# The channel stage of a 2-D Fourier mix computed once for both halves of its frequencies, with its product moved to GpSimd, inside a large transformer block in 32-bit arithmetic

## The chip, the cores and the metric

One core of a Trainium2 chip. The metric is the device time of one execution in microseconds (us). The engines are called as in the profile: PE (TensorE matmul), PEld (its weight loads), DVE (VectorE), ACT (ScalarE), POOL (GpSimd), SP (SyncE, which only issues transfers).

## The reference

One layer on 512 tokens of width 2048, with 256 context tokens. A normed and modulated input is projected to queries, keys, values, gates and the input of a Fourier branch; attention and Fourier mix run side by side, and their results are gated, merged, projected and normed. What the change touches is the Fourier branch:

```python
def _fourier_mix(u):                       # u: 512 tokens x 512 channels
    ug = u.reshape(b, n, 4, 128)           # four groups of 128 channels
    y = jnp.fft.fftn(ug, axes=(1, 3), norm="ortho").real
...
y_b = (_fourier_mix(u_b) * jax.nn.silu(z_b)) @ w_pb
```

`norm="ortho"` divides by the root of 512 x 128, which is 256. With A the transform over tokens (real part Ar, imaginary part Ai, up to sign), C and S the cosine and sine tables over channels, the real part at token frequency f is C Ar(f) - S Ai(f). The input is real, so at 512 - f it is C Ar(f) + S Ai(f).

## The kernel before

All matrix products are done on numbers split into a high part (rounded to the matmul's 32-bit input format) and a low part (the rest): `split_from` copies the high part on ACT and subtracts on DVE (L180, L181), and `mm3` issues three matmuls per product, high x high, high x low, low x high (L338, L339, L340). Most lines of the profile are such splits: `whi`, `wlo` are a weight's parts, `s` those of sums of the input's blocks (S4, Z and S among them), `ah`, `al` those of the token transform.

Weights are streamed. SP loads raw blocks `wr`; four chains R0 to R3 take further blocks by accumulating transfers on POOL's queue (L291) or by additions on DVE (`R<-R,wr`, L268). The program is a list of stages:

1. A start stage computes the Fourier input u and its gate input z_b with the weights as they arrive. `keep` puts the sums into the tile `part`; for z its rows 4 to 7, the last additions being L659.
2. The channel stage, the subject here. `halves` forms even and odd combinations of u's tokens. `tokens(g)`, one call for each of four channel groups, is the transform over tokens: 12 matmuls, 6 for even and 6 for odd frequencies, into PSUM tiles named `pb`, then the splits into `ah` and `al`. `positions(g)` is the transform over channels: 8 matmuls with `ah` and 4 with `al`, 256 columns each, into a PSUM tile `pd`. They are the cosine and sine terms of frequencies 0 to 255, and then once more those of 256 down to 1 with the sine's sign turned, for the other half. DVE multiplies the sum by 1/256 and by silu(z) in one instruction (L944), over z's place in `part`. `gate_b(g)` has made silu(z) before: a sigmoid on ACT (L949), a product on DVE (L950). Two stores (`b_d<-part`, L966) on POOL's queue then put the result in memory, for a later stage.
3. Eight groups of seven products each, P1, Q5, P2, Q6, P7, Q3, Q4 (a Strassen-like scheme: seven block products in place of eight). A product has four pieces; a piece is a weight block, split, and 12 matmuls into one of the PSUM pairs `x`, `y` or `banks`. `Group.run` goes through them. Groups 0 to 2 give queries and gates, group 3 uses a sigmoid for gates (L1182). The first product's sum is copied to `ev` by ACT (L1113); the tiles `ev` lie where `part` was.

The order of PE is written out by hand in the stages 1 and 2 (`tc.manual_schedule`); the other engines' orders come from a scheduler, held by `issue_after`, which `behind(...)` wraps: what stands inside it comes after the named instructions in its engine's order. In the channel stage, `split_piece` of the first weight blocks is put behind the low half of group g (`low[g]`), so that the splits of R0 to R2 stand between the groups' work.

Of the kernel before, what the change touches and what calls it, by code (L numbers as in the profile page):

```python
# [10 lines left out]
F32 = mybir.dt.float32  # L11
# [7 lines left out]
P = 128  # L19
# [25 lines left out]
RAW = 4  # L45

HL, MORE_HL = 3, 2
EVEN = 258

# [73 lines left out]
def block_kernel(ctx, tc, xT, ctx_rows, ctx_toks, x, c_row, w_ss, w_gate, vecs, qkg, rope, dft_c, dft_s,  # L123
# [32 lines left out]
    def uid(s):  # L156
        cnt[0] += 1
        return f"{s}{cnt[0]}"
# [20 lines left out]
    def split_from(src, hi, lo):  # L179
        first = nc.scalar.activation(hi, src, ACT.Copy)  # L180
        return first, nc.vector.tensor_tensor(lo, src, hi.bitcast(F32), op=ALU.subtract)  # L181
# [16 lines left out]
    def stream(key, src, *a, **k):  # L198
        todo.append(Piece(key, src if isinstance(src, list) else [src], *a, **k))
# [136 lines left out]
    def mm3(o, ah, al, bh, bl, start, stop, cont=False):  # L336

        nc.tensor.matmul(o, ah, bh, start=start, stop=False, skip_group_check=cont)  # L338
        nc.tensor.matmul(o, ah, bl, start=False, stop=False, skip_group_check=cont)  # L339
        nc.tensor.matmul(o, al, bh, start=False, stop=stop, skip_group_check=cont)  # L340
# [25 lines left out]

    for p in start_pieces():
        if p[2:5:2] == (KK - 4, 0):
            stream(("dfts", 0), dft_s[:, : 2 * EVEN], 2 * EVEN, 2, "raw")
# [143 lines left out]
    with tc.issue_after(nc.scalar.activation(ce, cvt, ACT.Exp, scale=-1.0).ins):  # L513
# [6 lines left out]
    fch = ppool.tile([P, 2, 3 * P], F32R, name="fch")  # L520
    fsq = [ppool.tile([P, 2, 2, EVEN], F32R, name="fsq0")]
    rx = pap.tile([P, T], F32, name="rx")
    wacc = bank3()
    def warm(n, src):
# [371 lines left out]
    fsq.append(fnp.tile([P, 2, 2, 256], F32R, name="fsq1"))  # L896
    split_table(1)

    def halves(a):
# [17 lines left out]

    def tokens(g):

        ah, al = (fnp.tile([P, 2, 257], F32R, tag=n, bufs=2, name=uid(n)) for n in ("ah", "al"))  # L920
        c = slice(P * g, P * g + P)
        for e in range(2):
            n = fsq[e].shape[-1]
            acc = bank()
            for a in range(2):
                mm3(acc[:, :n], uh[:, a, e, c], ul[:, a, e, c], fsq[e][:, 0, a, :], fsq[e][:, 1, a, :], a == 0, a == 1)
            k = slice(e, 257 - e, 2)
            low[g] = split_from(acc[:, :n].rearrange("p (r f) -> p r f", r=2), ah[:, :, k], al[:, :, k])[1]
        AH[g] = ah, al

    def positions(g):

        ah, al = AH.pop(g)
        acc = bank2()
        steps = [(256 * q, P * (r and 1 + q), (slice(0, 256) if q == 0 else slice(256, 0, -1)), r)
                 for q in range(2) for r in range(2)]
        for n, (o, t, k, r) in enumerate(steps):
            for m, i in enumerate((0, 1)):
                nc.tensor.matmul(acc[:, o : o + 256], fch[:, i, t : t + P], ah[:, r, k], start=n == m == 0, stop=False,
                                 skip_group_check=True)  # L940
# [3 lines left out]
        nc.vector.scalar_tensor_tensor(part[:, 4 + g, :], acc, 1.0 / 256.0, part[:, 4 + g, :], op0=ALU.mult, op1=ALU.mult)  # L944

    def gate_b(g):
        z = part[:, 4 + g, :]
        e = fnp.tile([P, T], F32, tag="sil", bufs=1, name=uid("e"))
        nc.scalar.activation(e, z, ACT.Sigmoid)  # L949
        nc.vector.tensor_tensor(z, z, e, op=ALU.mult)  # L950
# [444 lines left out]
    for g, kind in enumerate(KINDS):  # L1395
        if g == 3:
            jobs += [lambda: None] * 12 + [context_norm, lambda: None, lambda: None, context_spread]
        elif g == KV:
            while jobs:
                job()  # L1400
            assert not any(p[2] == "raw1" for e in ahead for p, _ in e.raws)
        elif g == KV + 1:
            qzs.close()
            gvs, gvp = region("gvp", "right", reuse_waits="tile")
            hl_pools += range(MORE_HL)
        group = Group(g, forms, new_ev, {"qz": qz_done, "kv": kv_done, "gate": gate_done}[kind], {"a": "x", "b": "y", "c": "x"})
        if g == KV:
            group.more = Context()
        for name in ONE_GROUP:
            if (g, name) in ((0, "Q4"), (KV + 1, "P1")):  # L1410
                assert not any(p[2] == "raw0" for e in ahead for p, _ in e.raws)
                load_row(int(g > 0))
            elif (g, name) == (1, "Q5"):
                silu_of_row(0, flat(new_ev()))
            if (g, name) == (0, "P7"):
                raw_pools.remove((rp, 1, "raw0", 1))
            if (g, name) == (0, "Q5"):
                more_hl.append(1)
# [24 lines left out]
    gvs.close()  # L1443
    evs.close()

# [543 lines left out]
def _constants():  # L1989
    pos = np.arange(T)  # L1990
    inv = (THETA ** (-np.arange(32, dtype=np.float64) / 32)).astype(np.float32)
    ang = np.stack([(pos // GRID).astype(np.float32)[:, None] * inv,
                    (pos % GRID).astype(np.float32)[:, None] * inv], axis=1)
    ang = ang.astype(np.float64)
    cos, sin = np.cos(ang), np.sin(ang)
    cos = np.stack([cos, cos], axis=2).reshape(T, HD)
    sin = np.stack([-sin, sin], axis=2).reshape(T, HD)
    rope = np.stack([cos, sin]).reshape(2, 4, P, HD).transpose(2, 0, 1, 3).astype(np.float32)
    a = 2 * np.pi * (np.outer(np.arange(P), np.arange(P)) % P) / P
    dft_c = np.concatenate([np.cos(a), -np.sin(a), np.sin(a)], axis=1).astype(np.float32)  # L2000
# [6 lines left out]
    dft_s = np.concatenate([table(np.arange(0, T // 2 + 1, 2)), table(np.arange(1, T // 2, 2))], axis=1)  # L2007
    return np.ascontiguousarray(rope), np.ascontiguousarray(dft_c), np.ascontiguousarray(dft_s)


# [58 lines left out]
```

## Time and profile before

| what | value |
| --- | --- |
| runs | 1290.64 us median of 3 (1289.82 to 1291.4) |
| profiled execution | 1290.61 us |
| its span | 1288.8 us, TensorE clock granted 0.998 of full speed |
| channel stage, PE | 144.60 to 156.13 us of the span |
| DMA | 319.14 MB, mean 248 GB/s |

The profile shows one execution. The span runs from its first to its last instruction; the runs' time has some 2 us more. In a line of the timeline stand the start, the duration, the engine, the line of code, the operation, what it writes and reads, its shape and, in brackets, how long the engine sat idle before and what ended that. A busy PE is not necessarily at its peak: matmuls are pipelined, so the time one takes of the engine is the distance between two starts, and the same holds for DVE and ACT.

### The profile page before, as it was taken

What the parts mean: (1) busy time and instruction counts of PE and PEld (TensorE: products, weight loads), DVE (VectorE), ACT (ScalarE), POOL (GpSimd) and SP (SyncE); (2) the same over time, 40 slices, a digit from 0 to 9 for tenths busy, and PEclk for the clock granted to TensorE, in tenths of its full rate; (3) what the DMA queues carried; (4) which work ended last, traced back from release to release, by engine and by line L of the source; (5) the groups of instructions that cost most, each with busy time, mean ns of one, the idle gap of its engine ahead of it and who ended that gap; (6) DMA issues with size and microseconds to landing.
All of it is one profiled execution on the core that took longest, in us unless ns stands there. A gap on an engine that the chain in (4) does not pass through costs nothing.

```text
span 1288.8 us, 17680 instructions
## 1 busy us (share of the span) xinstructions
PE 1272.9 (99%) x6586; PEld 1047.9 (81%) x6586; DVE 994.7 (77%) x1305; ACT 682.2 (53%) x1073; POOL 170.8 (13%) x222
## 2 busy tenths in 40 slices
PE   8999999999999999999999999999999999999997
PEld 5677887888888888888888888888888888888886
DVE  5767899889779787658587666788898777887677
ACT  5322654645556555444355544666667646464544
POOL 0000011111102011012031010012100211211210
PEclk9999999999999999999999999999999999999999
DMA  9998588888988988977879897578852989998986
GB/s 378 408 369 344 208 216 248 237 218 261 227 302 236 301 269 260 291 197 184 278 207 259 286 249 237 182 245 241 270 178 75 249 244 258 244 211 229 225 200 179
DMA packets 104486, 319.14 MB, mean 248 GB/s; under 512 B 9904, under 2 KB 33072, under 8 KB 100432
## 3 DMA queue, kind: packets, MB, share of 16 engines
q1 hardware_dynamic: 55056, 197.40, 42.3%
q0 software_dynamic: 27024, 98.19, 35.6%
q10 hardware_dynamic: 22320, 22.42, 5.1%
q8 instruction: 51, 0.84, 0.3%
q14 instruction: 35, 0.29, 0.1%
HBM read 283.36 MB, written 34.61 MB: 247 GB/s over the span
## 4 chain that ended last, share of the span: by engine, by line
PE 91%; DVE 3%; DMA 2%; ACT 2%; issue 1%; SPq 0%; ACTq 0%; DVEq 0%
PE banks L338 10%; PE banks L339 10%; PE banks L340 10%; PE x L340 9%; PE x L338 9%; PE x L339 9%; PE y L340 7%; PE y L339 7%; PE y L338 7%; PE banks L1543 2%; PE pd L566 2%; PE pb L338 1%; PE pb L339 1%; PE pb L340 1%; PE pc L338 1%; DMA wa<-in_w_ss 1%
## 5 line engine op out<-in xcount | busy, mean ns | idle before, releaser
L180 ACT ACTIVATE whi<-R 128x1024 fp32r<-128x1024 f32 x138 | 145.6, 1060 | 142.1 <-PE banks L340 55.3
L181 DVE TENSOR_TENSOR wlo<-R,whi 128x1024 fp32r<-128x1024 f32 x138 | 167.9, 1222 | 57.9 <-ACT whi L180 57.6
L181 DVE TENSOR_TENSOR wlo<-wr,whi 128x1024 fp32r<-128x1024 f32 (+1 forms) x122 | 147.2, 1214 | 63.1 <-ACT whi L180 63.1
L180 ACT ACTIVATE whi<-wr 128x1024 fp32r<-128x1024 f32 (+1 forms) x122 | 127.4, 1052 | 127.3 <-PE y L340 44.3
L338 PE MATMUL banks<-whi,s 128*128 128x512 f32 (+1 forms) x400 | 157.8, 394 | 0.9 <-DVE ev L1106 0.9
L339 PE MATMUL banks<-wlo,s 128*128 128x512 f32 (+1 forms) x400 | 155.8, 389 | 0.0
L340 PE MATMUL banks<-whi,s 128*128 128x512 f32 (+1 forms) x400 | 155.8, 389 | 0.0
L338 PE MATMUL x<-whi,s 128*128 128x512 f32 x352 | 137.1, 390 | 0.0
L340 PE MATMUL x<-whi,s 128*128 128x512 f32 x352 | 137.0, 389 | 0.0
L339 PE MATMUL x<-wlo,s 128*128 128x512 f32 x352 | 136.9, 389 | 0.0
L338 PE MATMUL y<-whi,s 128*128 128x512 f32 x316 | 123.1, 389 | 0.2 <-DVE cxe L1266 0.2
L339 PE MATMUL y<-wlo,s 128*128 128x512 f32 x316 | 123.1, 390 | 0.0
L340 PE MATMUL y<-whi,s 128*128 128x512 f32 x316 | 122.8, 389 | 0.0
L291 POOL DMA_DIRECT2D R<-in_w_g x64 | 56.0, 875 | 415.2 <-DVE wlo L181 212.6
L180 ACT ACTIVATE s<-wr 128x512 fp32r<-128x512 f32 (+2 forms) x93 | 60.9, 678 | 68.1 <-DMA wr<-cf_d 24.9
L338 PEld LDWEIGHTS banks<-whi,s 128*128 128x128 f32 x400 | 75.2, 188 | 16.6 <-DVE ev L1106 1.3
L181 DVE TENSOR_TENSOR s<-wr,s 128x512 fp32r<-128x512 f32 (+2 forms) x93 | 66.7, 750 | 28.3 <-ACT s L180 27.5
L340 PEld LDWEIGHTS banks<-whi,s 128*128 128x128 f32 x400 | 75.1, 188 | 15.3
L339 PEld LDWEIGHTS banks<-wlo,s 128*128 128x128 f32 x400 | 75.2, 188 | 13.6 <-DVE wlo L181 0.2
L340 PEld LDWEIGHTS x<-whi,s 128*128 128x128 f32 x352 | 66.1, 188 | 13.8
L339 PEld LDWEIGHTS x<-wlo,s 128*128 128x128 f32 x352 | 66.1, 188 | 13.7
L338 PEld LDWEIGHTS x<-whi,s 128*128 128x128 f32 x352 | 66.1, 188 | 13.6
(322 smaller groups left out, 2803.2 us busy)
## 6 DMA issues: line engine op xcount, KB each, us to landing
wr<-in_w_g SPq DMA_DIRECT2D x128, 512.0 KB, 5.8
R<-in_w_g POOLq DMA_DIRECT2D x64, 512.0 KB, 7.3
wa<-in_w_ss SPq DMA_DIRECT2D x31, 1024.0 KB, 9.7
R<-in_w_g SPq DMA_DIRECT2D x32, 512.0 KB, 6.0
wr<-in_w_gate SPq DMA_DIRECT2D x32, 512.0 KB, 5.1
wr<-in_w_o SPq DMA_DIRECT2D x24, 512.0 KB, 7.5
R<-in_w_o POOLq DMA_DIRECT2D x24, 512.0 KB, 9.2
wr<-in_w_pab SPq DMA_DIRECT2D x20, 512.0 KB, 6.0
```

What stands on the lines that cost most here:

```text
L180: first = nc.scalar.activation(hi, src, ACT.Copy)
L181: return first, nc.vector.tensor_tensor(lo, src, hi.bitcast(F32), op=ALU.subtract)
L291: nc.gpsimd.dma_start(chain[e.pc], e.nxt, accum_op=ALU.add)
L338: nc.tensor.matmul(o, ah, bh, start=start, stop=False, skip_group_check=cont)
L339: nc.tensor.matmul(o, ah, bl, start=False, stop=False, skip_group_check=cont)
L340: nc.tensor.matmul(o, al, bh, start=False, stop=stop, skip_group_check=cont)
L566: nc.tensor.matmul(acc[32 * j : 32 * j + 32], c2[:, n, :], w[:, k, :], start=n < 4, stop=n >= KK - 4)
L1543: nc.tensor.transpose(tp[:, k * P : (k + 1) * P], p[:, k * P : (k + 1) * P], ident)
```

## The change

- `positions` computes the cosine term and the sine term once, for 258 frequencies, in two accumulators `acc` (PSUM tiles `pb`): 4 matmuls with the high parts, then 2 with the low ones. ACT copies the sine term to `odd`; DVE subtracts it (columns 0 to 256) and adds it (255 columns, read backwards) to the cosine term, into `y`; GpSimd multiplies `y` by silu(z), over z's place.
- 1/256 goes into the cosine and sine tables, which lose the third block. Even and odd tables have 258 columns each.
- `tokens` takes its PSUM tiles from `bank2` (`pd`) and `bank3` (`pc`), where `positions` had `pd`.
- `gate_b` is one Silu on ACT, in place.
- The splits put behind `low[2]` and `low[3]` are now both behind `low[3]`, and the products P1 and Q5 of group 0 run in `behind((low[3],))`.

```diff
-EVEN = 258
+FREQ = 258
...
-            stream(("dftc", 0), dft_c, 3 * P, 1, "raw")
+            stream(("dftc", 0), dft_c, 2 * P, 1, "raw")
...
-            stream(("dfts", 1), dft_s[:, 2 * EVEN :], T, 2, "raw")
+            stream(("dfts", 1), dft_s[:, 2 * FREQ :], 2 * FREQ, 2, "raw")
...
-        ah, al = (fnp.tile([P, 2, 257], F32R, tag=n, bufs=2, name=uid(n)) for n in ("ah", "al"))
+        ah, al = (fnp.tile([P, 2, FREQ], F32R, tag=n, bufs=2, name=uid(n)) for n in ("ah", "al"))
         for e in range(2):
-            n = fsq[e].shape[-1]
-            acc = bank()
+            acc = (bank3 if e else bank2)()[:, :FREQ]
...
         ah, al = AH.pop(g)
-        acc = bank2()
-        steps = [(256 * q, P * (r and 1 + q), (slice(0, 256) if q == 0 else slice(256, 0, -1)), r)
-                 for q in range(2) for r in range(2)]
-        for n, (o, t, k, r) in enumerate(steps):
-            for m, i in enumerate((0, 1)):
-                nc.tensor.matmul(acc[:, o : o + 256], fch[:, i, t : t + P], ah[:, r, k], start=n == m == 0, stop=False,
+        acc = [bank()[:, :FREQ] for _ in range(2)]
+        for i, v in ((0, ah), (1, ah), (0, al)):
+            for r, o in enumerate(acc):
+                nc.tensor.matmul(o, fch[:, i, P * r : P * r + P], v[:, r, :], start=i == 0 and v is ah, stop=v is al,
                                  skip_group_check=True)
-        for n, (o, t, k, r) in enumerate(steps):
-            nc.tensor.matmul(acc[:, o : o + 256], fch[:, 0, t : t + P], al[:, r, k], start=False, stop=n == 3,
-                             skip_group_check=True)
-        nc.vector.scalar_tensor_tensor(part[:, 4 + g, :], acc, 1.0 / 256.0, part[:, 4 + g, :], op0=ALU.mult, op1=ALU.mult)
+        z = part[:, 4 + g, :]
+        y, odd = (fnp.tile([P, n], F32, tag=t, bufs=4, name=uid(t)) for t, n in (("y", T), ("odd", FREQ)))
+        nc.scalar.copy(odd, acc[1])
+        nc.vector.tensor_tensor(y[:, :257], acc[0][:, :257], odd[:, :257], op=ALU.subtract)
+        nc.vector.tensor_tensor(y[:, 257:], acc[0][:, 255:0:-1], odd[:, 255:0:-1], op=ALU.add)
+        nc.gpsimd.tensor_tensor(z, y, z, op=ALU.mult)
 
     def gate_b(g):
         z = part[:, 4 + g, :]
-        e = fnp.tile([P, T], F32, tag="sil", bufs=1, name=uid("e"))
-        nc.scalar.activation(e, z, ACT.Sigmoid)
-        nc.vector.tensor_tensor(z, z, e, op=ALU.mult)
+        nc.scalar.activation(z, z, ACT.Silu)
...
-        with behind((finals[-1], low[g])):
+        with behind((finals[-1], low[g if g < 2 else 3])):
...
-            group.run(name)
+            with behind((low[3],)) if (g, name) in ((0, "P1"), (0, "Q5")) else nullcontext():
+                group.run(name)
...
-    dft_c = np.concatenate([np.cos(a), -np.sin(a), np.sin(a)], axis=1).astype(np.float32)
+    dft_c = (np.concatenate([np.cos(a), np.sin(a)], axis=1) / 256.0).astype(np.float32)
```

What becomes of DVE's order in the channel stage: from its last addition to z to the second group's low halves. Before, each group's low halves stand behind a product with the sigmoid (`e`), and L944 multiplies `pd` by silu(z):

```order
L659 TENSOR_TENSOR part<-pc_1425,part 128x512
L950 TENSOR_TENSOR part<-part,e_1516 128x512
L181 TENSOR_TENSOR al_1440<-pb_1441,ah_1439 128x2x129
L181 TENSOR_TENSOR al_1440<-pb_1450,ah_1439 128x2x128
L950 TENSOR_TENSOR part<-part,e_1557 128x512
L181 TENSOR_TENSOR al_1460<-pb_1461,ah_1459 128x2x129
L181 TENSOR_TENSOR al_1460<-pb_1470,ah_1459 128x2x128
L181 TENSOR_TENSOR wlo_1554<-R_1339,whi_1553 128x1024
L944 SCALAR_TENSOR_TENSOR part<-pd_1482,part 128x512
```

After, in the same place (four low halves, a weight's split, then the subtraction and the addition of group 0):

```order
L659 TENSOR_TENSOR part<-pc_1425,part 128x512
L181 TENSOR_TENSOR al_1440<-pd_1441,ah_1439 128x258
L181 TENSOR_TENSOR al_1440<-pc_1450,ah_1439 128x258
L181 TENSOR_TENSOR al_1460<-pd_1461,ah_1459 128x258
L181 TENSOR_TENSOR al_1460<-pc_1470,ah_1459 128x258
L181 TENSOR_TENSOR wlo_1550<-R_1339,whi_1549 128x1024
L941 TENSOR_TENSOR y_1488<-pb_1480,odd_1489 128x257
L942 TENSOR_TENSOR y_1488<-pb_1480,odd_1489 128x255
```

The products with `e` and L944 are gone; the low halves follow each other directly, and the two y instructions stand where L944 stood.

POOL's order at that place, before:

```order
L766 DMA rot_d<-S_67 128x1024
L966 DMA b_d<-part 128x1024 x2
L1394 DMA qr<-rot_d 128x1024
L291 DMA R_1339<-in_w_g 128x1024
```

and after:

```order
L766 DMA rot_d<-S_67 128x1024
L943 TENSOR_TENSOR part<-y_1488,part 128x512
L943 TENSOR_TENSOR part<-y_1523,part 128x512
L963 DMA b_d<-part 128x1024
L943 TENSOR_TENSOR part<-y_1562,part 128x512
L943 TENSOR_TENSOR part<-y_1581,part 128x512
L963 DMA b_d<-part 128x1024
L1391 DMA qr<-rot_d 128x1024
L291 DMA R_1339<-in_w_g 128x1024
```

The four products stand in the queue ahead of the stores and of the transfers behind them.

DVE's order in the pieces of P7 and Q3 of group 0, some 50 us later. Names with their numbers (s40, s72: low halves for P7's last piece; s97, s128: for Q3's first; s333, in the changed order s341: the low half of the form S4). Before:

```order
L181 TENSOR_TENSOR s97_572<-wr317_1912,s95_571 128x2x256
L181 TENSOR_TENSOR s40_287<-wr316_1894,s38_286 128x2x256
L181 TENSOR_TENSOR s72_434<-wr316_1894,s70_433 128x2x256
L181 TENSOR_TENSOR s128_735<-wr317_1912,s126_734 128x2x256
L181 TENSOR_TENSOR wlo331_2022<-wr320_1932,whi330_2021 128x1024
L181 TENSOR_TENSOR s333_2038<-S30_67,s332_2037 128x1024
```

and after:

```order
L181 TENSOR_TENSOR s97_572<-wr325_1904,s95_571 128x2x256
L181 TENSOR_TENSOR s128_735<-wr325_1904,s126_734 128x2x256
L181 TENSOR_TENSOR s40_287<-wr324_1886,s38_286 128x2x256
L181 TENSOR_TENSOR s72_434<-wr324_1886,s70_433 128x2x256
L181 TENSOR_TENSOR wlo339_2014<-wr328_1924,whi338_2013 128x1024
L181 TENSOR_TENSOR s341_2030<-S30_67,s340_2029 128x1024
```

s128 has moved ahead of s40 and s72; the set and the last of them are the same.

More of the change, by code (lines that the diff above doesn't have):

```diff
@@ L368, in block_kernel @@
         if p[2:5:2] == (KK - 4, 0):
-            stream(("dfts", 0), dft_s[:, : 2 * EVEN], 2 * EVEN, 2, "raw")
-            stream(("dftc", 0), dft_c, 3 * P, 1, "raw")
+            stream(("dfts", 0), dft_s[:, : 2 * FREQ], 2 * FREQ, 2, "raw")
+            stream(("dftc", 0), dft_c, 2 * P, 1, "raw")
         elif p[2:5:2] == (KK - 4, 4):
-            stream(("dfts", 1), dft_s[:, 2 * EVEN :], T, 2, "raw")
+            stream(("dfts", 1), dft_s[:, 2 * FREQ :], 2 * FREQ, 2, "raw")
         stream(("start", p), w_start[p[0] : p[0] + P * p[1]].rearrange("(p c) -> p c", p=P), p[1], p[2 + 1])
@@ L519, in block_kernel @@
                             ce.rearrange("p (j k) -> p j k", j=2), op=ALU.mult)
-    fch = ppool.tile([P, 2, 3 * P], F32R, name="fch")
-    fsq = [ppool.tile([P, 2, 2, EVEN], F32R, name="fsq0")]
+    fch = ppool.tile([P, 2, 2 * P], F32R, name="fch")
+    fsq = [ppool.tile([P, 2, 2, FREQ], F32R, name="fsq0")]
     rx = pap.tile([P, T], F32, name="rx")
@@ L895, in block_kernel @@
     ul = fnp.tile([P, 2, 2, T], F32R, name="ul")
-    fsq.append(fnp.tile([P, 2, 2, 256], F32R, name="fsq1"))
+    fsq.append(fnp.tile([P, 2, 2, FREQ], F32R, name="fsq1"))
     split_table(1)
@@ L918, in tokens @@
     def tokens(g):
-        ah, al = (fnp.tile([P, 2, 257], F32R, tag=n, bufs=2, name=uid(n)) for n in ("ah", "al"))
+        ah, al = (fnp.tile([P, 2, FREQ], F32R, tag=n, bufs=2, name=uid(n)) for n in ("ah", "al"))
         c = slice(P * g, P * g + P)
         for e in range(2):
-            n = fsq[e].shape[-1]
-            acc = bank()
+            acc = (bank3 if e else bank2)()[:, :FREQ]
             for a in range(2):
-                mm3(acc[:, :n], uh[:, a, e, c], ul[:, a, e, c], fsq[e][:, 0, a, :], fsq[e][:, 1, a, :], a == 0, a == 1)
-            k = slice(e, 257 - e, 2)
-            low[g] = split_from(acc[:, :n].rearrange("p (r f) -> p r f", r=2), ah[:, :, k], al[:, :, k])[1]
+                mm3(acc, uh[:, a, e, c], ul[:, a, e, c], fsq[e][:, 0, a, :], fsq[e][:, 1, a, :], a == 0, a == 1)
+            k = slice(e, FREQ, 2)
+            low[g] = split_from(acc.rearrange("p (r f) -> p r f", r=2), ah[:, :, k], al[:, :, k])[1]
         AH[g] = ah, al
@@ L2005, in table @@
         return v.reshape(2, P, -1).transpose(1, 0, 2).reshape(P, -1)
-    dft_s = np.concatenate([table(np.arange(0, T // 2 + 1, 2)), table(np.arange(1, T // 2, 2))], axis=1)
+    dft_s = np.concatenate([table(np.arange(e, FREQ, 2)) for e in range(2)], axis=1)
     return np.ascontiguousarray(rope), np.ascontiguousarray(dft_c), np.ascontiguousarray(dft_s)
```

## The prediction

> **What bounds the kernel now.** I read the page first: busy times, then the chain that ended last.
>
> ```profile
> PE 1272.9 (99%) x6586; PEld 1047.9 (81%) x6586; DVE 994.7 (77%) x1305; ACT 682.2 (53%) x1073; POOL 170.8 (13%) x222
> PE 91%; DVE 3%; DMA 2%; ACT 2%; issue 1%; SPq 0%; ACTq 0%; DVEq 0%
> ```
>
> Over the whole span TensorE (PE) is the bound, so work taken from it should come off the end, unless another engine is the bound where the work goes. I therefore took the busy times by stretches: the first begins in the channel stage, the second follows it.
>
> ```profile
> core 0: us, PE busy (x) PEld busy (x) DVE busy (x) ACT busy (x) POOL busy (x), PEclk, DMA share, GB/s
> 145.80:212.60 66.80, 65.89 (x330) 55.42 (x328) 66.45 (x86) 38.79 (x64) 11.04 (x14) 1.00 0.70 186
> 212.60:235.00 22.40, 22.36 (x99) 18.51 (x100) 20.05 (x22) 11.37 (x15) 0.00 (x0) 1.00 0.80 271
> ```
>
> In the 66.80 us from 145.80 VectorE (DVE) has 0.35 us idle and PE 0.91. Behind 212.60 DVE has 2.35 idle and PE next to none. So both are full up to 212.6, and the timeline of PE there tells which waits for which; the bracket is its idle time and what ended it. The DVE row is the low half that the second wait ends on.
>
> ```profile
> 209.16 0.50 PE L339 MATMUL x<-s,s 128*128 128x512 f32 x1 [0.71 <-DVE s L181]
> 212.64 0.50 PE L340 MATMUL y<-s,s 128*128 128x512 f32 x1 [0.24 <-DVE s L181]
> 211.36 1.23 DVE L181 TENSOR_TENSOR s<-S,s 128x1024 fp32r<-128x1024 f32 x1
> ```
>
> PE waits there twice, both times for DVE, and 0.71 + 0.24 is all of its 0.91 idle but rounding. The low half of the form ends at 211.36 + 1.23 = 212.59 and the matmul starts at 212.64. Hence DVE's unbroken row from 145.8 to 212.6 sets the time at which PE passes 212.6, and from there PE runs without idle: what DVE gains or loses by then stays to the end, and what PE alone gains before it turns into waiting.
>
> **PE's part.** Each group now has 24 matmuls in the stage (12 in `tokens`, 12 in `positions`), 96 in all.
>
> ```profile
> 144.60 0.28 PE L338 MATMUL pb<-fsq,uh 128*128 128x258 f32 x1
> 144.72 0.28 PE L339 MATMUL pb<-fsq,uh 128*128 128x258 f32 x1
> 147.47 1.12 PE L939 MATMUL pd<-ah,fch 128*128 128x256 f32 x8
> 156.13 0.40 PE L338 MATMUL x<-whi,s 128*128 128x512 f32 x1
> ```
>
> The pitch is 144.72 - 144.60 = 0.12; 96 x 0.12 = 11.52, and the stage takes 156.13 - 144.60 = 11.53. The changed `positions` has 6, so 72 matmuls: 8.64 us, and P1 can start at 153.24, 2.88 earlier (258 columns have the pitch of 256). By the above this lead is worth nothing unless DVE arrives sooner too.
>
> **DVE's part.**
>
> ```profile
> 145.20 0.69 DVE L659 TENSOR_TENSOR part<-pc,part 128x512 f32<-128x512 f32 x1
> 145.80 0.69 DVE L950 TENSOR_TENSOR part<-part,e 128x512 f32<-128x512 f32 x1
> 146.40 0.76 DVE L181 TENSOR_TENSOR al<-pb,ah 128x258 fp32r<-128x258 f32 x2
> 148.53 1.22 DVE L181 TENSOR_TENSOR wlo<-R,whi 128x1024 fp32r<-128x1024 f32 x1
> 149.66 0.69 DVE L944 SCALAR_TENSOR_TENSOR part<-pd,part 128x512 f32<-128x512 f32 x1
> 150.27 0.43 DVE L181 TENSOR_TENSOR al<-pb,ah 128x258 fp32r<-128x258 f32 x1
> 150.62 0.68 DVE L950 TENSOR_TENSOR part<-part,e 128x512 f32<-128x512 f32 x1
> 157.09 0.69 DVE L944 SCALAR_TENSOR_TENSOR part<-pd,part 128x512 f32<-128x512 f32 x1
> 157.69 1.22 DVE L181 TENSOR_TENSOR s<-Z,s 128x1024 fp32r<-128x1024 f32 x1
> ```
>
> What an instruction takes of DVE is its pitch, start to start: 0.60 for 512 columns (145.20 to 145.80), 1.13 for 1024 (148.53 to 149.66), and for 258 columns 0.35 (150.27 to 150.62) or 0.33 (the pair spans 0.76, one 0.43); I take 0.34. Removed are four L944 (149.66 the first, 157.09 the last) and the three L950 that lie in the stretch: 7 x 0.60 = 4.20. (A fourth ran earlier, where DVE waits.) Added are a subtraction and an addition for each group, 257 and 255 columns: 8 x 0.34 = 2.72. Work falls by 1.48.
>
> But `s<-Z`, the first instruction behind the stage, doesn't come 1.48 sooner. From 145.80 to 157.69 are 11.89 us; by pitches the work before is 3 x 0.60 + 8 x 0.34 + 3 x 1.13 + 4 x 0.60 + 1.13 = 11.44, idle 0.45. The products with the sigmoid were the work that covered DVE's waits for the high halves.
>
> ```profile
> 145.54 0.39 ACT L180 ACTIVATE ah<-pb 128x258 fp32r<-128x258 f32 x1
> 146.24 0.40 ACT L180 ACTIVATE ah<-pb 128x256 fp32r<-128x256 f32 x1 [0.31 <-PE pb L340]
> 146.58 0.64 ACT L949 ACTIVATE e<-part 128x512 f32<-128x512 f32 x1
> ```
>
> Walking the changed order with these durations: DVE is free at 145.80, the first low half starts at 146.08 (waits 0.28); the second's high half stands behind the last silu on ScalarE (ACT), which can't start before L659's end at 145.89, so it starts at 146.97 (0.55); the next two wait 0.12 and 0.38 for PE's sums. Later a low half of group 1's sums 0.10, and the last one, of group 3, 0.39 for PE's last sums, which end at 152.52. New waits 1.82, work 9.96: `s<-Z` at 157.58, a gain of 0.11. Were all waits covered, it would be 1.93.
>
> **The products on GpSimd (POOL).** Four of 128x512, both inputs in SBUF, written over z. The trace has no such instruction. Nearest in size is a memset of that tile; nearest in kind are small ones.
>
> ```profile
> L533 POOL MEMSET s<- 128x512 f32 x1 | 0.5, 531 | 0.0
> 198.62 0.20 POOL L1196 TENSOR_SCALAR small<-small 128x8 f32<-128x8 f32 x1 [1.44 <-ACT y L1208]
> 664.53 2.29 POOL L1196 TENSOR_SCALAR small<-small 128x8 f32<-128x8 f32 x1
> 664.08 1.22 DVE L268 TENSOR_TENSOR R<-R,wr 128x1024 f32<-128x1024 f32 x1
> 665.55 1.22 DVE L268 TENSOR_TENSOR R<-R,wr 128x1024 f32<-128x1024 f32 x1
> 386.72 1.08 POOL L1196 TENSOR_SCALAR small<-small 128x2 f32<-128x2 f32 x1 [32.50 <-DVE small L1311]
> 386.53 1.22 DVE L268 TENSOR_TENSOR R<-R,wr 128x1024 f32<-128x1024 f32 x1
> 387.67 1.22 DVE L181 TENSOR_TENSOR wlo<-R,whi 128x1024 fp32r<-128x1024 f32 x1
> 388.92 1.23 DVE L268 TENSOR_TENSOR R<-R,wr 128x1024 f32<-128x1024 f32 x1
> ```
>
> The memset writes one stream in 0.53. Two streams read through one port would take 1.06 (I take it), three streams in turn 1.59; the lower end is 0.53.
>
> The other rows show that POOL and DVE get in each other's way. The same POOL instruction takes 0.20 at 198.62 and 2.29 at 664.53, where DVE ran two-input SBUF instructions from 664.08 on; it ends at 666.82, with the one that began at 665.55. At 386.72 it ends at 387.80, just behind the one begun at 386.53, so it slipped in between two of them, and DVE's start at 388.92 is 0.12 later than 387.67 + 1.13. The Trainium skill has the rule for it, page "SBUF — State Buffer", section "Who interferes with whom": GpSimd shares one port pair with DVE, held exclusively, so that a DVE instruction with both inputs in SBUF and GpSimd's shut each other out. The trace agrees for POOL (0.20 against 2.29); by the rule the sum is 1292.2, without it 1290.5.
>
> Worked out from rows: DVE's low halves of weights (`wlo<-R,whi`) and `R<-R,wr` read SBUF twice, its low halves of sums and the new y read PSUM once. Product 0 (from 150.3) stands beside reads of PSUM: nothing. Product 1, 151.8 to 152.9, holds the split due at 152.8 by 0.1. Product 2, 154.7 to 155.8, holds the one due at 155.3 by 0.5. Product 3 finds DVE without a gap and costs it a whole product, 1.06. Together 1.7 at 1.06 each; 0.5 at 0.53; 3.2 at 1.59 (0.6 + 1.0 + 1.59).
> The page "GPSIMD Engine Reference" of the Trainium skill, section "3.1 Elementwise — side-by-side cycle accounting", has 4497 ns for such an instruction of 2048 columns; a quarter, 1.12, is an estimate from it, and the sum by it would be 0.1 higher. No run here shows it.
>
> The additions read 255 columns backwards, of which DVE has no row. Nearest is a forward one, 0.34; at the upper end I let it double, 4 x 0.34 = 1.4 more. I take nothing, since PE's reversed operands in the x8 group above cost nothing (1.12 - 0.28 = 7 x 0.12).
>
> **The store behind the products.**
>
> ```profile
> 153.66 0.53 POOL L966 DMA_DIRECT2D b_d<-part  x1 [74.20 <-DVE part L944]
> b_d<-part POOLq DMA_DIRECT2D x2, 512.0 KB, 3.4
> 167.22 1.02 ACT L1113 COPY ev<-x 128x1024 f32<-128x1024 f32 x1 [1.66 <-PE x L340]
> ```
>
> b_d goes out in two stores, the second behind products 2 and 3 on POOL's queue, and `ev`, first written at 167.22, lies in `part`'s memory, so this copy waits for the landing. Product 3 at about 156.5, ending 157.6, plus 0.53, plus 3.4: 161.5, before the copy even if that comes 2.88 sooner. Behind it in POOL's queue are the load of `qr` and the accumulating loads of R, with some us to spare.
>
> **The rest.**
>
> ```profile
> 138.43 1.28 ACT L949 ACT_TABLE_LOAD   x1
> 419.24 1.03 ACT L1182 ACTIVATE ev<-x 128x1024 f32<-128x1024 f32 x1 [0.63 <-PE x L340]
> 427.20 0.39 PE L338 MATMUL y<-s,s 128*128 128x512 f32 x1
> 144.60:156.10 11.50, 11.50 (x97) 11.50 (x96) 11.22 (x21) 8.48 (x16) 0.53 (x1) 1.00 0.20 79
> ```
>
> Silu takes the sigmoid's place in this first table load; the gates' sigmoid at 419.24 then needs one of its own, 1.28, of which 0.63 lies in a wait. The other 0.65 delays the split behind it on ACT, one of the pieces that PE starts to multiply at 427.20, some 7 us later: nothing; uncovered it is +0.65. ACT gets four copies of 258 columns, 4 x 0.39, and its queue has room (8.48 of the stage's 11.50 us busy, the last row). The narrower cosine table and two more columns of a sine table change loads on SP's queue by under a hundredth: nothing. The splits of R0 to R2 behind the stage's last low half come later on DVE, before PE needs them, behind the 36 matmuls with which P1 starts; if one is late, PE spends its 2.88 lead there. The row behind 157.7 holds the same DVE work up to the same form, the one that ends at 212.59 now; what is exchanged in between only changes places.
>
> **Sum.** The profiled execution is at 1290.61, the median at 1290.64, so they need no correction. 1290.6 - 0.1 + 1.7 = **1292.2**. Ends of this case: no lock cost and all waits covered 1288.7, no lock cost 1290.5; the long product 1290.6 - 0.1 + 3.2 = 1293.7, with doubled backward reads 1295.1.
>
> **Rivals.**
> *Nothing of the lock* (products slip in while DVE reads PSUM or waits): 1290.5, down to 1288.7. For it, two of four products are nearly covered; against it, DVE has no gap behind 155.
>
> *Faster: PE's lead arrives.* If the two late low halves at 209 and 212 were late by their order and not by the amount of DVE's work, the changed order (s97 and s128 ahead of s40) frees PE there: 1290.6 - 2.88 = 1287.7. For it, PE's 99%; against it, 66.45 of 66.80. It decides from 2.6 us of DVE work less or moved behind 212.6.
>
> *Slower: product 3 starves.* If it loses every gap between DVE's two-input instructions, as it did twice at 664.53, the store, the copy to `ev` and the weight split behind it on ACT stop, until DVE itself runs dry waiting for that split, where today copy and high half end: 167.22 + 1.02 + about as much, 169.3. Then product 1.06, issue 0.53, landing 3.4, copy and high half 1.0 each give 176.3: +7, 1297.6. Against it, 386.72. It decides if product 3 starts after about 160.5.
>
> **Chances.** Forecast's case 0.62 (0.45 of it below 1293.2), no lock 0.15, PE's lead 0.12, starved 0.11. A measurement of this kernel tells apart about 0.2%, 2.6 us. Faster 0.12; same 0.45 + 0.15 = 0.60; slower 0.17 + 0.11 = 0.28. The range takes the first three: 1287.6 to 1295.1.
>
> **What would show it.** P1's first matmul near 153.2; `s<-Z` on DVE at 159 (157.6 without lock); POOL's products longer than 1.06 or DVE gaps beside them; PE waiting 4 to 5 us for DVE in this stretch, mostly before the form's matmul near 214. The forecast is wrong if PE passes that matmul before 212, or if the first copy to `ev` waits for the store.

## The result, and the profile after

1293.07 us median of 18 runs (1292.44 to 1295.01) against 1290.92 of the kernel before (18 runs): ratio 1.0017, 95% interval 1.0010 to 1.0024. The whole interval lies above 1: the kernel becomes slower by about 2.2 us (0.17%), 0.9 more than the forecast of 1292.2. The profiled execution took 1293.05. Medians are over all executions, here and below.

The page of the changed kernel, busy times and chain:

```profile
PE 1271.3 (98%) x6562; PEld 1046.4 (81%) x6562; DVE 994.2 (77%) x1305; ACT 682.5 (53%) x1078; POOL 175.6 (14%) x226
PE 90%; DVE 6%; ACT 1%; issue 1%; DMA 1%; SPq 0%; DVEq 0%; ACTq 0%
```

PE has 1.6 us less to do and the kernel is longer: DVE's share of the chain rose from 3% to 6%. The busy times by stretches (columns as before the change) say where:

```profile
145.80:214.70 68.90, 63.91 (x301) 53.04 (x300) 67.74 (x86) 38.58 (x65) 17.60 (x18) 0.98 0.67 177
214.70:240.00 25.30, 25.30 (x113) 20.96 (x112) 22.12 (x24) 12.03 (x15) 0.00 (x0) 1.00 0.84 276
```

In the first stretch PE now idles 5.0 us instead of 0.9, and its granted clock (the 0.98) is no longer whole. Behind it PE is full, as before. PE's waits from the stage to 260 us (total, number of times, longest):

```profile
PE x L339 <- DVE wlo L181: 2.4, 1, 2.4
PE y L339 <- DVE s L181: 2.1, 1, 2.1
PE x L339 <- DVE s L181: 0.5, 1, 0.5
```

All three are for DVE. DVE's timeline in the stage, from the last addition to z, shows what became of it:

```profile
144.61 0.68 DVE L659 TENSOR_TENSOR part<-pc,part 128x512 f32<-128x512 f32 x1
145.64 0.43 DVE L181 TENSOR_TENSOR al<-pd,ah 128x258 fp32r<-128x258 f32 x1 [0.35 <-ACT ah L180]
146.44 0.43 DVE L181 TENSOR_TENSOR al<-pc,ah 128x258 fp32r<-128x258 f32 x1 [0.37 <-ACT ah L180]
...
149.58 0.41 DVE L942 TENSOR_TENSOR y<-pb,odd 128x255 f32<-128x255 f32 x1
149.91 0.42 DVE L181 TENSOR_TENSOR al<-pd,ah 128x258 fp32r<-128x258 f32 x1
...
152.48 1.47 DVE L181 TENSOR_TENSOR wlo<-R,whi 128x1024 fp32r<-128x1024 f32 x1
155.20 1.94 DVE L181 TENSOR_TENSOR wlo<-R,whi 128x1024 fp32r<-128x1024 f32 x1
157.06 2.32 DVE L268 TENSOR_TENSOR R<-R,wr 128x1024 f32<-128x1024 f32 x1
159.30 2.35 DVE L181 TENSOR_TENSOR s<-Z,s 128x1024 fp32r<-128x1024 f32 x2
```

The forecast's waits for high halves are there (0.35, 0.37). Three instructions that took 1.22 before now take 1.47, 1.94 and 2.32: 0.25 + 0.72 + 1.10 = 2.07 more. They are those beside which GpSimd multiplies; POOL's timeline (two pairs):

```profile
150.31 2.56 POOL L943 TENSOR_TENSOR part<-y,part 128x512 f32<-128x512 f32 x2 [71.24 <-PE pb L936]
154.77 3.52 POOL L943 TENSOR_TENSOR part<-y,part 128x512 f32<-128x512 f32 x2 [1.03 <-DVE y L942]
158.59 0.59 POOL L963 DMA_DIRECT2D b_d<-part  x1 [0.30 <-POOL part L943]
```

A product alone takes 1.28 (2.56 for two). Further on, the low half of the form S4 on DVE, and PE around the two later waits:

```profile
212.75 1.21 DVE L181 TENSOR_TENSOR s<-S,s 128x1024 fp32r<-128x1024 f32 x1
...
209.93 0.50 PE L339 MATMUL y<-s,s 128*128 128x512 f32 x1 [2.10 <-DVE s L181]
211.13 0.76 PE L339 MATMUL x<-s,s 128*128 128x512 f32 x1 [0.47 <-DVE s L181]
211.69 0.63 PE L340 MATMUL x<-s,s 128*128 128x512 f32 x1
212.12 0.63 PE L338 MATMUL x<-s,s 128*128 128x512 f32 x1
...
215.34 0.39 PE L340 MATMUL y<-s,s 128*128 128x512 f32 x1
```

The low half ends at 212.75 + 1.21 = 213.96, but the matmul that needs it starts at 215.34: this time PE is late, not DVE. From 211.69 its matmuls stand 0.43 apart instead of 0.23. The stretches show why, in the column PEclk (the third number from the end, 1.00 or 0.50):

```profile
160.00:163.42 3.42, 1.55 (x7) 0.94 (x5) 3.42 (x4) 0.54 (x1) 0.55 (x1) 1.00 0.84 273
163.42:166.83 3.41, 2.85 (x12) 2.35 (x13) 3.41 (x4) 2.10 (x3) 0.90 (x1) 1.00 0.88 308
207.79:211.20 3.41, 0.84 (x4) 0.37 (x3) 3.41 (x6) 2.11 (x3) 1.29 (x2) 1.00 0.06 7
211.20:214.62 3.42, 3.42 (x8) 2.71 (x9) 3.42 (x4) 0.63 (x1) 0.14 (x1) 0.50 0.99 163
215.20:217.20 2.00, 2.00 (x11) 1.65 (x10) 1.26 (x2) 1.66 (x3) 0.00 (x0) 1.00 0.88 330
```

The clock is granted at half for 3.41 us, from 211.20 to 214.62, behind the waits of 2.10 and 0.47. Behind the wait of 2.42, at 163.98, it stays whole. This is called the half clock below.

### The profile page after: what moved, and what is told of

It is laid out like the page before. It is cut to its first block, busy times and chain, and to the rows that moved or that the text cites. A ratio compares the mean times of both kernels' runs of the same rounds, so it can differ in the third digit from the quotient of the medians.

```text
span 1291.3 us, 17644 instructions
## 1 busy us (share of the span) xinstructions
PE 1271.3 (98%) x6562; PEld 1046.4 (81%) x6562; DVE 994.2 (77%) x1305; ACT 682.5 (53%) x1078; POOL 175.6 (14%) x226
## 4 chain that ended last, share of the span: by engine, by line
PE 90%; DVE 6%; ACT 1%; issue 1%; DMA 1%; SPq 0%; DVEq 0%; ACTq 0%
PE banks L338 10%; PE banks L339 10%; PE banks L340 10%; PE x L339 8%; PE x L340 8%; PE x L338 8%; PE y L340 7%; PE y L338 7%; PE y L339 7%; PE banks L1541 2%; PE pd L566 2%; PE pc L338 1%; DVE wlo L181 1%; PE pb L338 1%; PE pc L340 1%
```

## The experiments

DVE's row is compared by one number: the time from the start of the last L659 to the start of S4's low half. Before it is 211.36 - 145.20 = 66.16, after the change 212.75 - 144.61 = 68.14, +1.98. (Executions reach the stage up to 0.8 us apart, so absolute times aren't compared.) PE is compared in the same way, at one matmul well behind S4: the 5000th from the last, which is the same piece of work in every kernel. Before and after it starts here:

```profile
258.56 0.39 PE L338 MATMUL x<-whi,s 128*128 128x512 f32 x1
261.13 0.39 PE L338 MATMUL x<-whi,s 128*128 128x512 f32 x1
```

From the last L659 these are 258.56 - 145.20 = 113.36 and 261.13 - 144.61 = 116.52, +3.16. The next column says where the profile has the half clock in this stretch: at S4's waits, at an earlier wait, or not at all. These three columns are of one profiled execution each. The mean clock is over all executions of a kernel, less that of the kernel before on the same chip; one stretch of 3.4 us at half clock is 1.7 of 1290, 0.0013. It is a rough measure: single executions of one kernel lie between 0.995 and 0.999, and some profiles have a half clock near the span's start too (8 to 15 us).

| kernel | time, median minus before | ratio, 95% interval | DVE to S4's low half | PE behind S4 | half clock | mean clock |
| --- | --- | --- | --- | --- | --- | --- |
| changed | +2.15 | 1.0010 to 1.0024 | +1.98 | +3.16 | at S4 | |
| e1 without the product | +0.79 | 0.9997 to 1.0014 | -0.06 | +1.14 | at S4 | -0.0011 |
| e2 product on DVE | +2.68 | 1.0010 to 1.0027 | +3.01 | +3.00 | none | +0.0001 |
| e3 PE padded | +3.12 | 1.0012 to 1.0030 | +1.92 | +1.91 | earlier | -0.0008 |
| e4 Silu alone | -0.97 | 0.9980 to 0.9997 | -0.74 | -0.74 | none | -0.0001 |
| e5 PE padded twice | +2.44 | 1.0007 to 1.0025 | +2.00 | +2.09 | none | -0.0002 |
| e6 products added to before | +1.46 | 1.0004 to 1.0021 | +1.99 | +2.00 | none | -0.0002 |
| e7 changed, again | +2.25 | 1.0010 to 1.0028 | +2.55 | +2.58 | earlier | -0.0014 |
| e8 no y | -0.66 | 0.9985 to 1.0003 | -1.25 | -0.01 | at S4 | -0.0011 |
| e9 splits undone | +2.01 | 1.0007 to 1.0025 | +2.53 | +2.54 | earlier | -0.0018 |
| e10 two products on DVE | +2.77 | 1.0012 to 1.0030 | +2.11 | +2.10 | none | -0.0003 |
| e11 waits filled | +2.76 | 1.0010 to 1.0027 | +1.88 | +3.08 | at S4 | -0.0012 |
| e12 Silu, first split ahead | -2.06 | 0.9971 to 0.9988 | -2.35 | -1.75 | none | +0.0002 |

The two columns in the middle settle what the half clock is worth in one execution. Where it stands at S4's waits (changed, e1, e8, e11), PE is 3.16 - 1.98 = 1.18, 1.20, 1.24 and 1.20 us later than DVE's row explains. Where it stands at an earlier wait or is absent, PE and DVE agree to 0.1: PE then only has less time to spend waiting. (In e12 PE is 0.60 behind DVE without it: there PE itself is the bound.)

### The product left out

```diff
-        y, odd = (fnp.tile([P, n], F32, tag=t, bufs=4, name=uid(t)) for t, n in (("y", T), ("odd", FREQ)))
+        y, odd = z, fnp.tile([P, FREQ], F32, tag="odd", bufs=4, name=uid("odd"))
...
-        nc.gpsimd.tensor_tensor(z, y, z, op=ALU.mult)
```

`y` is written straight over z, and the kernel leaves out the product with silu(z).

> The changed kernel without the product with silu(z): DVE writes y over z's place, nothing runs on GpSimd in the stage (the product is left out of the result). Theory A (GpSimd's products hold up DVE's two-input instructions, in the changed kernel's trace by 0.25 + 0.72 + 1.10 = 2.07 us; PE then waits so much that its clock is halved for 3.4 us, another 1.3): DVE passes s<-Z 2.1 sooner, no half clock, 1293.1 - 2.1 - 1.3 = 1289.7. Rival B (the lock counts, the half clock is hidden behind DVE): 1291.0. Rival C (it is DVE's new waits for high halves in the stage, the lengthened rows are covered elsewhere): 1293.1, no change.

1291.68 (1289.80 to 1294.56). The same three instructions, and S4's low half:

```profile
145.16 0.68 DVE L659 TENSOR_TENSOR part<-pc,part 128x512 f32<-128x512 f32 x1
153.10 1.22 DVE L181 TENSOR_TENSOR wlo<-R,whi 128x1024 fp32r<-128x1024 f32 x1
155.56 1.22 DVE L181 TENSOR_TENSOR wlo<-R,whi 128x1024 fp32r<-128x1024 f32 x1
156.69 1.22 DVE L268 TENSOR_TENSOR R<-R,wr 128x1024 f32<-128x1024 f32 x1
211.26 1.22 DVE L181 TENSOR_TENSOR s<-S,s 128x1024 fp32r<-128x1024 f32 x1
```

All three are back at 1.22, and DVE is where the forecast put it without the lock: -0.06 against before (forecast -0.11). So the lengthening is GpSimd's, and the rest of the change leaves DVE's row as it was. The time is not back, though: 2.0 above theory A's 1289.7, which only the fastest execution comes near, and 0.7 above B. Theory A took the half clock to go with the product, and it didn't: PE, 2.3 us ahead of DVE at 208, waits for it there, the profiled execution has the half clock behind it, and PE is 1.14 late behind S4 though DVE is on time.

### The product on DVE

```diff
-        nc.gpsimd.tensor_tensor(z, y, z, op=ALU.mult)
+        nc.vector.tensor_tensor(z, y, z, op=ALU.mult)
```

> The changed kernel with the same four products on DVE. Theory A: DVE's work rises by 4 x 0.60 = 2.4 and loses the 2.07 of waiting for GpSimd: +0.3, 1293.4, the half clock stays. If GpSimd's products cost DVE nothing: +2.4, 1295.5.

1293.57 (1292.43 to 1295.06), near the 1293.4 of theory A and far from 1295.5: moving the product to GpSimd saves the kernel next to nothing. The agreement is partly luck: DVE's row is 1.0 later than in the changed kernel, not 0.3, since DVE waits 1.12 for a high half (`wlo` at 167.21) that ACT gives it; and theory A's half clock is absent from the profile.

### GpSimd's products by themselves

```diff
         nc.vector.scalar_tensor_tensor(part[:, 4 + g, :], acc, 1.0 / 256.0, part[:, 4 + g, :], op0=ALU.mult, op1=ALU.mult)
+        gp = fnp.tile([P, T], F32, tag="gp", bufs=4, name=uid("gp"))
+        nc.gpsimd.tensor_tensor(gp, part[:, 4 + g, :], part[:, 4 + g, :], op=ALU.mult)
```

> The kernel before with four GpSimd products of 128x512 added, each squaring a finished row of part into a tile that nobody reads; nothing else. Theory A (each holds DVE's two-input instructions, for up to its own 1.28 us): DVE's row and the end are later by 1.3 to 4 us, taken as 2.0: 1292.9. If GpSimd's products do not hold up DVE, and it was only the changed order: 1290.9.

1292.64 (1292.29 to 1294.30), ratio 1.0004 to 1.0021: four products that nobody waits for, but for the stores behind them, cost the kernel before 1.5 us. DVE's and POOL's timelines:

```profile
150.62 1.50 DVE L952 TENSOR_TENSOR part<-part,e 128x512 f32<-128x512 f32 x1
154.78 1.61 DVE L181 TENSOR_TENSOR wlo<-R,whi 128x1024 fp32r<-128x1024 f32 x1
158.65 3.44 DVE L268 TENSOR_TENSOR R<-R,wr 128x1024 f32<-128x1024 f32 x2
150.54 1.04 POOL L946 TENSOR_TENSOR gp<-part 128x512 f32<-128x512 f32 x1 [71.08 <-DVE part L944]
157.09 1.94 POOL L946 TENSOR_TENSOR gp<-part 128x512 f32<-128x512 f32 x1 [1.26 <-DVE part L944]
```

1.50 for 0.68, 1.61 for 1.22 and 3.44 for 2.35: 0.82 + 0.39 + 1.09 = 2.3 us, of which DVE's row shows 1.99 at S4 (0.18 less waiting at the stage's end is one piece of the difference). And the product at 157.09 takes 1.94 instead of 1.04: each side holds up the other.

### PE padded, once and twice, and the changed kernel again

```diff
             ah, al = self.forms[form][j]
+            for _ in range(4 if start and (self.g, form) == (0, "S3") else 0):
+                nc.tensor.matmul(a[:, t, :], ah[:, s], w[0][:, j % 2, :], start=True, stop=False, skip_group_check=True)
             mm3(a[:, t, :], ah[:, s], al[:, s], w[0][:, j % 2, :], w[1][:, j % 2, :],
```

This is e3's edit; e5 asks for `"A11"` (product P1) as well as `"S3"` (product P7). e7 has no edit.

> The changed kernel with eight more matmuls on PE: at the start of product P7 of group 0 the first matmul of each of the two sums is issued four more times (each starts the sum anew, so the result is the same), 8 x 0.23 = 1.8 us of work, some 8 us ahead of PE's second wait for DVE (2.10 us). Theory A: the wait falls to 0.3, the clock stays whole, and the kernel becomes faster by 1.3 us though PE has 1.8 more to do: 1291.8. Rival B (the half clock is hidden): 1293.1. If PE's work counted: 1294.9.

1294.01 (1291.88 to 1295.40). Theory A's 1291.8 is the fastest of eleven executions, not the median. The profiled one (1295.40) had the half clock elsewhere, behind the first wait (2.40), where the pad doesn't reach. At S4 the pad did its work: PE passes there with DVE (+1.91, against +3.16 in the changed kernel's profile). What it won is lost later, 1.1 us of it in a wait for DVE at 627 that the changed kernel's profile doesn't have.

> The changed kernel with sixteen more matmuls on PE: the first matmul of both sums is issued four more times at the start of P1 and of P7 of group 0 (the result is the same), 8 x 0.23 = 1.8 us ahead of each of PE's two long waits for DVE (2.42 at 163.98, 2.10 at 209.93). Theory A (the half clock behind these waits costs the changed kernel 1.1 us): both waits fall to about half a us, the clock stays whole, 1293.1 - 1.1 = 1292.0 though PE has 3.6 us more to do. Rival B (DVE alone sets the time, the half clock is hidden or rare): 1293.1. If PE's work counted: 1296.7.

1293.62 (1292.64 to 1294.77). With both waits shortened (1.8 and 0.5 in the profile) the mean clock is that of the kernel before, to 0.0002, and PE passes S4's low half as soon as DVE allows (+2.09). But the end isn't earlier: the profiled execution, 1294.77, loses 0.7 and 1.8 us in waits for DVE at 626 and 854. Theory A's 1292.0 is refuted for the end, and PE's work doesn't count either (1296.7). Whether the pads cause these later waits isn't shown.

> The changed kernel once more, beside the others: 1293.1 by every theory. It gives the scatter, and whether the half clock behind 211 is there in another execution.

1293.43 (1293.07 to 1294.96). The half clock is there again, at another place, behind the first wait (two rows of PE, then two stretches):

```profile
164.63 0.50 PE L339 MATMUL x<-wlo,s 128*128 128x512 f32 x1 [2.42 <-DVE wlo L181]
...
165.65 0.63 PE L339 MATMUL x<-wlo,s 128*128 128x512 f32 x1
...
161.77:165.19 3.42, 1.00 (x4) 0.50 (x4) 3.42 (x4) 1.16 (x3) 0.55 (x1) 1.00 0.69 204
165.19:168.60 3.41, 3.41 (x9) 2.64 (x8) 3.41 (x4) 0.94 (x1) 0.90 (x1) 0.50 1.05 293
```

So the half clock recurs in the changed kernel: it is in both of its profiles, and the mean clock of its eleven executions, 0.0014 lower, agrees with one such stretch in each, though it doesn't prove it. Where it falls decides what it costs. In the first profile it lay at S4's waits and cost 1.18; here it lay at the first wait, PE waits less for DVE at S4, and behind S4 PE is as late as DVE (+2.58 and +2.55).

The wait is 2.42 in both profiles; what differs is where it lies. The stretches of half clock begin and end on a grid of 3.41 us (in the changed kernel's first profile the clock is whole from 13.23 to 211.20, which is 58 x 3.413). Here the whole wait falls into one window of this grid, 161.77 to 165.19. There it was cut by a border at 163.42, with PE idle for 1.86 us ahead of it and 0.56 behind.

### Neither product nor y

```diff
-        y, odd = (fnp.tile([P, n], F32, tag=t, bufs=4, name=uid(t)) for t, n in (("y", T), ("odd", FREQ)))
+        odd, even = (fnp.tile([P, FREQ], F32, tag=t, bufs=4, name=uid(t)) for t in ("odd", "even"))
...
-        nc.vector.tensor_tensor(y[:, :257], acc[0][:, :257], odd[:, :257], op=ALU.subtract)
-        nc.vector.tensor_tensor(y[:, 257:], acc[0][:, 255:0:-1], odd[:, 255:0:-1], op=ALU.add)
-        nc.gpsimd.tensor_tensor(z, y, z, op=ALU.mult)
+        nc.scalar.copy(even, acc[0])
```

The kernel leaves out the stage's last step.

> The changed kernel without the last step of the stage: neither subtraction, addition nor product (ACT copies both sums out of PSUM, z stays silu(z)). DVE has 2.7 us less to do than without the product alone, of which 0.3 goes into a wait for PE's last sums. Theory A (PE's lead of 2.88 is worth something as soon as DVE comes sooner too): 1290.9 - 2.4 = 1288.5. If PE's matmuls in this stage counted for nothing: 1290.9.

1290.52 (1289.37 to 1292.13), interval of the ratio 0.9985 to 1.0003: not told apart from no change, 2.0 above theory A. DVE's row is 1.25 shorter, not 2.4: it now waits for the high halves of groups 2 and 3 (0.31, 1.00 and 0.30), that is for PE's sums. DVE has less to do, but not enough of it ahead of these sums to come sooner. And the 1.25 don't reach PE: the half clock at S4 takes 1.24, and PE is where it was before (-0.01).

### The splits put back

```diff
-        with behind((finals[-1], low[g if g < 2 else 3])):
+        with behind((finals[-1], low[g])):
...
-            with behind((low[3],)) if (g, name) in ((0, "P1"), (0, "Q5")) else nullcontext():
-                group.run(name)
+            group.run(name)
```

> The changed kernel with its moved weight splits put back: each behind the low half of its own group as before, and P1 and Q5 no longer behind the stage's last low half. Theory A (GpSimd's hold on DVE is the loss): a split now fills the 0.29 us that the last low half waits, the lengthened instructions stay: 1293.2 - 0.3 = 1292.9. Rival D (the splits' new places are the loss): 1291.1.

1292.59 (1291.91 to 1294.67): near theory A's 1292.9 and far from rival D's 1291.1. The splits' places are not the loss. On DVE the lengthened instructions have only moved: a split of 2.18 for 1.22 and two sums R + wr of 3.90 for 2.35, 2.5 us together, where DVE's row is 2.53 later.

### Two products on DVE, and the waits filled

```diff
-        nc.gpsimd.tensor_tensor(z, y, z, op=ALU.mult)
+        (nc.gpsimd if g < 2 else nc.vector).tensor_tensor(z, y, z, op=ALU.mult)
```

> The changed kernel with the products of groups 2 and 3 on DVE and those of 0 and 1 on GpSimd. Theory A: DVE gets 2 x 0.60 = 1.20 of work and loses the 0.72 + 1.10 = 1.82 of waiting that products 2 and 3 cost it: -0.6, 1292.6. If GpSimd's products cost DVE nothing: 1294.4.

1293.35 (1291.65 to 1294.59): a miss. DVE's row at S4 is as late as in the changed kernel (+2.11), though in the stage the products cost what was expected. What it gained there (the second split is back at 1.21) it lost in one wait of its own, for ACT:

```profile
155.84 1.21 DVE L181 TENSOR_TENSOR wlo<-R,whi 128x1024 fp32r<-128x1024 f32 x1
166.26 1.23 DVE L181 TENSOR_TENSOR wlo<-R,whi 128x1024 fp32r<-128x1024 f32 x1 [0.67 <-ACT whi L180]
```

For e11, besides, e9's edit, and R0's split ahead of the stage's low halves:

```diff
-        with behind((finals[-1], low[g if g < 2 else 3])):
-            for e in ahead[:g]:
+        with behind((finals[-1], low[g])[: 1 + (g > 0)]):
+            for e in ahead[: max(1, g)]:
```

> The run before it (products 2 and 3 on DVE), with the splits put back and R0's split ahead of the stage's first low half, so that DVE does this split and the sum R0 + wr, 2.26 us, while ACT makes the high halves. If the waits for high halves (0.35 + 0.37 + 0.20 + 0.28 at the start, 0.29 at the end, some 0.2 between) are a part of the changed kernel's loss: 1.4 sooner than 1292.6, 1291.2. If they are covered elsewhere: 1292.6.

1293.34 (1291.23 to 1295.40): a miss too. The waits in the stage are gone from DVE's timeline, but product 1 now holds the split at 150.92 (2.10 for 1.22), and later DVE waits for ACT's high halves instead, 0.38 + 0.26 + 1.05:

```profile
150.92 2.10 DVE L181 TENSOR_TENSOR wlo<-R,whi 128x1024 fp32r<-128x1024 f32 x1
184.97 0.69 DVE L181 TENSOR_TENSOR s<-R,s 128x512 fp32r<-128x512 f32 x1 [0.38 <-ACT s L180]
185.93 1.23 DVE L181 TENSOR_TENSOR s<-S,s 128x1024 fp32r<-128x1024 f32 x1 [0.26 <-ACT s L180]
188.81 0.69 DVE L181 TENSOR_TENSOR s<-R,s 128x512 fp32r<-128x512 f32 x1 [1.05 <-ACT s L180]
```

On top of this PE waits 2.46 for a high half of ACT, at 210.68, with the half clock behind it. DVE's unbroken row in the profile before was thus no proof that DVE alone sets the pace: in these orders, what DVE gained went into waits for ACT.

### Silu alone, and a version that beats both

```diff
-        e = fnp.tile([P, T], F32, tag="sil", bufs=1, name=uid("e"))
-        nc.scalar.activation(e, z, ACT.Sigmoid)
-        nc.vector.tensor_tensor(z, z, e, op=ALU.mult)
+        nc.scalar.activation(z, z, ACT.Silu)
```

> The kernel before with one part of the change alone: gate_b is one Silu on ACT, the sigmoid and DVE's product go. DVE loses three 0.60 us instructions in the stretch, 1.8. Theory A's bookkeeping (DVE's row sets the end; products with the sigmoid covered waits for high halves, so some of the gain turns into waits): 1290.9 - 0.8 = 1290.1, between 1289.1 and 1290.9. If PE were the bound: 1290.9, no change.

1289.92 (1288.91 to 1290.98), interval 0.9980 to 0.9997: faster, by 0.97 where 0.8 was expected; DVE's row and PE behind S4 are both 0.74 earlier.

e12 is this and, in the kernel before, e11's line that puts R0's split first:

> The kernel before with Silu alone and R0's split ahead of the stage's first low half. DVE's waits there (0.21 + 0.37 + 0.18 + 0.28 us with Silu alone) are filled, DVE is 1.0 sooner; but with Silu alone PE's waits for DVE in the stretch are down to 0.2, so PE's own work is the bound: 1289.9 - 0.2 = 1289.7. If DVE still set the end: 1288.9.

1288.52 (1287.86 to 1290.79), interval 0.9971 to 0.9988: faster than before by 2.1 us and than the changed kernel by some 4. It is below even the 1288.9. DVE, the first rows of its timeline and S4's low half, and the busy times up to there:

```profile
145.08 0.68 DVE L659 TENSOR_TENSOR part<-pc,part 128x512 f32<-128x512 f32 x1
145.68 1.21 DVE L181 TENSOR_TENSOR wlo<-R,whi 128x1024 fp32r<-128x1024 f32 x1
146.81 1.08 DVE L181 TENSOR_TENSOR al<-pb,ah 128x258 fp32r<-128x258 f32 x3
147.81 1.21 DVE L268 TENSOR_TENSOR R<-R,wr 128x1024 f32<-128x1024 f32 x1
208.89 1.21 DVE L181 TENSOR_TENSOR s<-S,s 128x1024 fp32r<-128x1024 f32 x1
145.80:210.90 65.10, 65.10 (x329) 55.67 (x328) 65.09 (x82) 38.66 (x63) 11.01 (x14) 1.00 0.77 197
```

No wait is left on DVE in the stage, nor on PE in the whole stretch. That PE could win only 0.2 was wrong: the brackets count less than a wait costs. In the kernel before PE goes from a start at 208.06 to one at 209.16, 0.87 over its pitch of 0.23, where the bracket has 0.71, and its next matmul, 0.34 on, loses another 0.11. In e4 the starts around PE's two waits (207.71, 208.22, 208.56 and 211.08, 211.70, 212.03) lose 0.89 in all, where the only bracket has 0.23; e12 wins this back, and PE is 1.0 earlier than in e4.

## Why the prediction was right

- **DVE sets the end: right as to the forecast, with a limit.** PE's 2.88 turned into waits (forecast 4 to 5 us, measured 2.42 + 2.10 + 0.47 = 4.99); P1 starts at 152.99 (153.2). Nearly half of the waiting, the 2.42, comes earlier than forecast, at 163.98 for a weight's split. The rival "PE's lead arrives" is refuted. There are two limits: in e10 and e11 ACT takes over where DVE is relieved, and PE's own clock can make it late (the sum, below).
- **DVE's work and new waits: right.** Forecast a gain of 0.11 at `s<-Z`. With the product left out (e1) it comes 157.82 - 145.16 = 12.66 behind the last L659, where it was 157.69 - 145.20 = 12.49, so 0.17 later; at S4 the row is 0.06 shorter. The waits that the brackets show in the changed kernel are 0.35 + 0.37 + 0.20 + 0.28 + 0.29 = 1.49, where 1.82 were forecast.
- **The products on GpSimd: right in kind, too small in size.** Forecast 0.1 + 0.5 + 1.06 = 1.7, measured 0.25 + 0.72 + 1.10 = 2.07, because a product takes 1.28 and not 1.06. `s<-Z` starts at 159.30 (159). The rule of the Trainium skill cited in the prediction (page "SBUF — State Buffer", section "Who interferes with whom") holds in both directions here: DVE's instruction took 2.32 instead of 1.22, and in e6 POOL's 1.94 instead of 1.04. Its estimate from the page "GPSIMD Engine Reference", 1.12, was nearer to 1.28 than the 1.06 taken (in all three terms it would have added 0.2, not 0.1). "Nothing of the lock" is refuted by e1 and e6.
- **Starved product: didn't happen.** Product 3 got in behind one DVE instruction, its store started at 158.59, and no copy to `ev` waited for it: the store takes about 3.1 us to land, and the copy starts at 166.89, once PE has the sum.
- **Backward reads, 257 and 255 columns:** 0.33 us each (149.58 to 149.91). The value taken, nothing extra, was right.
- **The sum.** With 2.07 in place of 1.7 it is 1292.6; 1293.07 was measured. What was left out is the half clock: PE's waits halve its clock for 3.41 us, which costs 1.2 us where it falls on S4's waits (changed, e1, e8, e11) and nothing where it falls earlier (e3, e7, e9). For the profiled execution this closes the account: DVE +1.98, the half clock +1.18, -0.14 from there to the end, and 0.59 because this execution reaches L659 that much sooner, make 2.43, and 1293.05 - 1290.61 is 2.44. That the forecast came within 0.9 is partly luck, since such terms partly cancel. How often the half clock falls on S4's waits isn't known, so its share of the median stays open. e3 and e5, built to take it away, did so at S4 but lost it again further on (waits at 627, and at 626 and 854). One later wait seems to belong to the change: PE waits 0.4 to 1.1 us for the load `s<-yb_d` near 1125 in nine of the ten profiles of the changed kernel and its variants (not in e5), and in none of the four of the kernel before and its variants (e4, e6, e12). Why isn't shown.
- **The second table load:** it stands at 421.19 in the changed kernel, 1.28 us, and PE has no wait near it, as forecast.

## What to carry to other kernels

Before work is taken from the busiest engine, look in the stretch where it lies for the engine whose row has no gap: here PE was at 99% of the span, and yet 2.9 us less for it was worth nothing, while 1.8 us less for DVE (one Silu for a sigmoid and a product) and a split moved into its waits were worth 2.1. GpSimd is no free place for a product of two SBUF operands beside DVE instructions of that kind: price it at up to its own length on DVE. And a wait on PE has a price beyond its length, which can depend on where it falls.

## What the runs showed of the hardware that was not expected

- A GpSimd product of 128x512 in 32 bits takes 1.28 us with two different operands and 1.04 with one operand twice. Beside DVE instructions with two SBUF operands it took up to 2.27 (changed kernel, from 156.0) and 1.94 (e6).
- PE's clock is granted in windows of 3.41 us. In each profile the stretches at half clock begin and end on one grid of this width (the last ends with the span). Over all 14 profiles, from the stage to 1275 us, PE's idle time in one window went with the clock of the window behind it: all five windows with 1.89 us idle or more (1.89, 2.04, 2.40, 2.42, 2.57) were followed by half clock, two of the five with 1.6 to 1.87 were, and none with 1.46 or less. So the same wait can halve the clock in one execution and not in the next. The Trainium skill, page "TensorE: Matmul & The Clock Gate", section "Part 1: The HAM clock gate (the "warmup" mystery)", gives about 3.4 us of idling as what halves the clock; the length of the slow stretch agrees with that window, the waits seen here were shorter, and the measurement decides.
- The first matmul behind a wait takes 0.50 instead of 0.39, and the one behind it starts 0.34 later instead of 0.23, with the clock whole.
